# The end of the mixer: order of the vector work and of product 7's matmuls

## Chip, cores and metric

The kernel runs on one core of one Trainium2 chip. The metric is the device time of one execution in microseconds (us); three runs of the kernel before gave 1850.46 us as the median, with 1850.1 as the lowest and 1854.3 as the highest. Engines are named as the profile names them: PE is the tensor engine's matmuls, PEld its weight loads, DVE the vector engine, ACT the scalar engine, POOL GpSimd, SP the engine that issues most transfers.

## The reference

Two layers of an encoder trunk run over 512 tokens of width 1024, in float32. Each layer is a half-step feed-forward block, a mixer, and a second half-step feed-forward block:

```python
for l in range(DEPTH):
    x = x + 0.5 * swiglu(rms_norm(x, ffn1_norm[l]), ffn1_w_in[l], ffn1_w_out[l])
    x = x + mixer(rms_norm(x, mix_norm[l]), mix_w_in[l], mix_gate_bias[l], na_rpb[l],
                  na_w_out[l], f_w_out[l], mix_w_o[l])
    x = x + 0.5 * swiglu(rms_norm(x, ffn2_norm[l]), ffn2_w_in[l], ffn2_w_out[l])
return rms_norm(x, final_norm)
```

The mixer ends in `(g_na * y_na + g_f * y_f) @ w_o`, a 512x1024 by 1024x1024 product whose result is added to `x`. That product, and the start of the feed-forward block behind it, are what the change touches.

## The kernel before

**Numbers.** A float32 operand is split into a high part (ACT rounds a copy) and a low part (DVE subtracts the high part from the source, line 202 for weights, line 333 for activations). A product of two operands is three matmuls: high by high, low activation by high weight, high activation by low weight.

**Products.** `w_o` is multiplied by one level of Strassen's method, in seven half-size products numbered 1 to 7, in the order 1, 5, 2, 6, 7, 3, 4. Each has two row blocks (two PSUM banks, for example wA of product 1) and reads its weights in two granules of 128x1024 from a stream. A granule is 12 matmuls in `product`: through `late_low` the eight that read the high weight `whi` come first (lines 521 and 522, the second of them with the activation's low part) and the four that read the low weight `wlo` come last (line 524). In the first granule both row blocks run mixed, in the last one bank 0 is finished before bank 1. Products 6, 7 and 4 accumulate in the banks of product 1 (`pa`, tiles wA), product 3 in those of product 5 (`pb`, wB); product 2 has `pc` (wC).

**Adding to x.** `put(ps, i, j, sign, bs)` adds half of a bank to a quarter of `x` for the row blocks `bs`: one DVE instruction of 128x512 for a bank (line 1835). Product 7 accumulates on top of product 6 in wA, so each of its banks is free for PE only when `put` has read product 6 out of it. Product 7's activation is the difference `m01`, which DVE makes at line 1808; `parts` makes its high part m7h on ACT and its low part m7l on DVE. Product 3's parts are m3h and m3l, product 4's m4h and m4l.

**Order.** A scheduler places the instructions on every engine by priorities of its own, except where the code asks for the written order. In the block around products 6 and 7 PE and DVE keep it: `put` of pc's bank 0, product 6, `put` of both banks of product 6, `put` of pc's bank 1, product 7. Every engine runs its own queue in order.

**Weights ahead.** `whi` and `wlo` have three buffers each, so a granule's parts are made at most three granules ahead of PE. Raw weights have nine buffers in the feed-forward stage; SP issues their loads in one queue (line 148), and each waits for the buffer's last reader. Some weights are sums: of two raws on DVE (line 172), or made by a POOL transfer that accumulates onto a raw that has landed (lines 158 and 204).

**Behind the mixer.** `nxt.quad(i, j)` transposes quarters of `x` on PE (tiles tr, line 433), ACT scales them (xr) and makes the high part (xh), DVE the low part (xl, line 438). `nxt.squares` sums squares on ACT (junk). The feed-forward block's `first_block` then needs combinations of the quarters (line 616) and their parts: t5h and t5l for its product 5, t6h and t6l for its product 6. Its norm factor r is spread over the partitions by two POOL transfers, row<-r (line 512) and R<-row (line 514); DVE first reads R at line 826.

Of the kernel before, what the change touches and what calls it, by code (L numbers as in the profile page):

```python
# [31 lines left out]
AHEAD = 2  # L32
# [59 lines left out]
def encoder_kernel(  # L92
# [3 lines left out]
    V, S, G, PE = nc.vector, nc.scalar, nc.gpsimd, nc.tensor  # L96
# [15 lines left out]
    def slot(dt=F32, s="k", shape=(4, 256)):  # L112
        return kp.tile([P, *shape], dt, tag="k", name=nm(s), bufs=23)
# [8 lines left out]
    def pair(s="ps"):  # L122
        return [bank(s), bank(s)]
# [159 lines left out]
    class Stream:  # L283
# [32 lines left out]
        def next(self, ahead=AHEAD):  # L316
            self.prep(self.pos + 1 + ahead)
            it = self.items[self.pos]
            self.pos += 1
            return it.out  # L320
# [9 lines left out]
    def split(hi, lo, src, scale=None):  # L330
        if scale is None:
            S.activation(hi, src, AF.Copy)
            V.tensor_tensor(lo, src, hi.bitcast(F32), ALU.subtract)
            return
        S.activation(hi, src, AF.Copy, scale=scale)
        V.scalar_tensor_tensor(lo, src, scale, hi.bitcast(F32), ALU.mult, ALU.subtract)
# [180 lines left out]
    def late_low(parts, again=False):  # L517


        for ps, lh, ll, rh, _, start, _ in parts:  # L520
            PE.matmul(ps, lh, rh, start=start, stop=False, skip_group_check=again)  # L521
            PE.matmul(ps, ll, rh, start=False, stop=False, skip_group_check=again)  # L522
        for ps, lh, _, _, rl, _, stop in parts:
            PE.matmul(ps, lh, rl, start=False, stop=stop, skip_group_check=again)  # L524

    def product(ps, acts, kts, start, stop=True, again=False, hook=None, by_block=False, ahead=AHEAD):

        h, l, off = acts  # L530
        n = (len(kts) + 1) // 2

        def granule(i, w, b):
            res = []
            for k, kt in enumerate(kts[2 * i : 2 * i + 2]):
                c, z = slice(off + b * P, off + (b + 1) * P), slice(k * T, (k + 1) * T)
                res.append((
                    ps[b], h[:, kt, c], l[:, kt, c], w[0][:, z], w[1][:, z], start and i + k == 0,
                    stop and 2 * i + k == len(kts) - 1,
                ))  # L540
            return res

        if by_block:
            w = [ws.next() for _ in range(n)]
            for b in range(2):
                for i in range(n):
                    late_low(granule(i, w[i], b), again)
            return
        for i in range(n):
            w = ws.next(AHEAD if i < n - 1 and ahead else ahead)  # L550
            if i < n - 1:
                late_low(granule(i, w, 0) + granule(i, w, 1), again)
            else:
                late_low(granule(i, w, 0), again)
                late_low(granule(i, w, 1), again)
            if hook and i == 0:
                hook()
# [19 lines left out]
    def combo(dst, in0, in1, op, s):  # L577
        V.tensor_tensor(dst, in0, in1, op)
        return parts(dst, s)

    def parts(src, s):
        h, l = slot(F32R, s + "h"), slot(F32R, s + "l")
        split(h, l, src)
        return h, l, 0

    K4 = list(range(4))
# [41 lines left out]
    def stage_ffn(norm, nxt, late):  # L628
# [177 lines left out]
        def two(settle):  # L806

            pa = pair("A")
            product(pa, acts[1], K4, True)
            s1 = snap(pa)  # L810
            if settle:
                settle_at()
            pb = pair("B")
            product(pb, acts[5], K4, True)
            return pa, pb, s1, snap(pb)

        def second(s1):
            pc = pair("C")
            product(pc, acts[2], K4, True)
            less(pc, s1)  # L820
# [265 lines left out]
    def stage_mixer(l, norm, nxt):  # L1086
# [452 lines left out]
        with tc.manual_schedule(engines={mybir.EngineType.DVE, mybir.EngineType.Activation}):  # L1539
            with tc.manual_schedule(engines={mybir.EngineType.PE}):  # L1540
                u, k1, pa, sb, acts4 = proj_UV()
# [83 lines left out]
                low = ws.prep_high()  # L1625
# [95 lines left out]
                t12, _ = next(first)  # L1721
# [3 lines left out]
        acts = {1: (hx[0], lx[0], 0), 2: (hx[1], lx[1], 0), 3: (hx[1], lx[1], 256), 4: (hx[0], lx[0], 256)}  # L1725

        def high(src, s):
            h = slot(F32R, s + "h")
            S.activation(h, src, AF.Copy)
            return h  # L1730

        def low(h, src, s):
            l_ = slot(F32R, s + "l")
            V.tensor_tensor(l_, src, h.bitcast(F32), ALU.subtract)
            return h, l_, 0

        with tc.manual_schedule(engines={mybir.EngineType.DVE, mybir.EngineType.Activation}):
# [10 lines left out]
            w = [ws.next(), ws.next()]  # L1748
# [38 lines left out]
        m00, m01 = mq[0, 0], mq[0, 1]  # L1787
        a1 = parts(m00, "m1")
        a5 = combo(m00, m00, m01, ALU.subtract, "m5")
        w = [ws.next(), ws.next()]  # L1790
# [3 lines left out]
        pa = pair("wA")  # L1794
# [5 lines left out]
        pb = pair("wB")  # L1800
        product(pb, a5, K4, True)
        put(pb, 1, 1, -1)
        m11 = slot(F32, "mq")
        joined_words(m11, t11)
        a6 = combo(m00, m00, m11, ALU.add, "m6")
        pc = pair("wC")
        product(pc, a2, K4, True)
        V.tensor_tensor(m01, m01, m11, ALU.subtract)
        a7 = parts(m01, "m7")
        a3 = parts(m11, "m3")  # L1810
        with tc.manual_schedule(engines={mybir.EngineType.PE}):
            with tc.manual_schedule(engines={mybir.EngineType.DVE}):
                put(pc, 0, 0, 1, (0,))
                product(pa, a6, K4, False, again=True, ahead=1)
                put(pa, 0, 1, -1)
                put(pc, 0, 0, 1, (1,))
                product(pa, a7, K4, False, again=True)
                a4 = combo(m10, m10, m00, ALU.subtract, "m4")
            nxt.squares(0, 0)
            put(pa, 1, 1, 1)  # L1820
            nxt.squares(1, 1)
            nxt.quad(0, 0)
            product(pb, a3, K4, False, again=True)
        put(pb, 0, 1, 1)
        nxt.squares(0, 1)
        product(pa, a4, K4, False, again=True, hook=lambda: nxt.quad(0, 1))
# [4 lines left out]
    def put(ps, i, j, sign, bs=(0, 1)):  # L1831

        for b in bs:
            v = x[:, 2 * j + b, i * T : (i + 1) * T]
            V.scalar_tensor_tensor(v, ps[b], 0.5 * sign, v, ALU.mult, ALU.add)
# [43 lines left out]
    for l in range(L):  # L1879
        nxt = Norm(3 * l + 1)  # L1880
        stage_ffn(norm, nxt, False)
        norm, nxt = nxt, Norm(3 * l + 2)
        stage_mixer(l, norm, nxt)
        norm, nxt = nxt, Norm(3 * l + 3)
        stage_ffn(norm, nxt, l == L - 1)
        norm = nxt
# [148 lines left out]
```

## Time and profile before

| what | us |
|---|---|
| median of three runs | 1850.46 |
| the profiled execution | 1851.89 |
| its span, first to last instruction | 1850.1 |
| PE busy in the span | 1834.9 |
| DVE busy in the span | 1602.8 |
| ACT busy in the span | 1318.2 |

The profile is of one execution; a row of its timeline has the start from the span's beginning, the duration, the engine, the line and the operation with the tile written and the tiles read, and in brackets the idle time just before it with what released it. A row with x2 or more holds a group of like instructions. The mixer's end lies at about 573 to 605 us in the first layer and at about 1490 to 1522 us in the second, 917.5 us later.

### The profile page before, as it was taken

How to read it: one execution, taken by the hardware profiler on the slowest of the kernel's cores; microseconds unless marked ns; L12 is line 12 of the kernel's file. 1: busy time of each engine (PE TensorE's matmuls, PEld its weight loads, DVE VectorE, ACT ScalarE, POOL GpSimd, SP SyncE). 2: the span in 40 equal slices, each digit the busy share in tenths (PEclk: the TensorE clock that was granted, in tenths of full speed). 3: DMA queues.
4: the chain of work that ended last, by engine and by line, in shares of the span. 5: the costliest groups of instructions: out<-in, count | busy, mean ns of one | idle time of the engine just before them, and what ended most of it. 6: DMA issues, size and time to landing. Idle time of an engine off the chain costs nothing.

```text
span 1850.1 us, 24544 instructions
## 1 busy us (share of the span) xinstructions
PE 1834.9 (99%) x8834; PEld 1527.5 (83%) x8834; DVE 1602.8 (87%) x1942; ACT 1318.2 (71%) x1781; POOL 175.6 (9%) x215
## 2 busy tenths in 40 slices
PE   9999999999999999999999999999999999999998
PEld 7888888888887888888888888888888878888876
DVE  7878899787989987889998888997869899888898
ACT  6777875668576777786666778766776786677865
POOL 0001011100111010001010100101001111100010
PEclk9999999999999999999999999999999999999999
DMA  9898798934887788979888987998258878898795
GB/s 299 227 235 222 189 272 272 230 110 127 240 228 183 180 206 242 216 205 261 246 200 212 232 217 195 278 292 206 69 186 213 228 182 184 231 218 220 199 279 148
DMA packets 202538, 396.77 MB, mean 214 GB/s; under 512 B 108016, under 2 KB 108144, under 8 KB 202416
## 3 DMA queue, kind: packets, MB, share of 16 engines
q1 hardware_dynamic: 173072, 295.28, 49.8%
q0 software_dynamic: 28912, 99.38, 30.4%
q8 instruction: 69, 1.13, 0.2%
q10 hardware_dynamic: 432, 0.55, 0.1%
q14 instruction: 53, 0.43, 0.1%
HBM read 367.88 MB, written 2.11 MB: 200 GB/s over the span
## 4 chain that ended last, share of the span: by engine, by line
PE 90%; DVE 5%; DMA 3%; issue 2%; ACT 1%; POOL 0%; SPq 0%; DVEq 0%; POOLq 0%; ACTq 0%
PE A L521 10%; PE A L524 10%; PE A L522 10%; PE o L524 6%; PE o L521 5%; PE o L522 5%; PE B L521 5%; PE B L522 5%; PE B L524 5%; PE ps L326 4%; PE ps L327 3%; PE ps L328 3%; DMA raw<-in_wst_dram 3%; PE C L522 3%; PE C L521 3%; PE C L524 3%
## 5 line engine op out<-in xcount | busy, mean ns | idle before, releaser
L202 DVE TENSOR_TENSOR wlo<-raw,whi 128x1024 fp32r<-128x1024 f32 (+1 forms) x532 | 628.6, 1192 | 176.4 <-ACT whi L199 172.5
L199 ACT ACTIVATE whi<-raw 128x1024 fp32r<-128x1024 f32 (+1 forms) x532 | 544.0, 1033 | 263.9 <-PE A L522 54.0
L158 POOL DMA_DIRECT2D raw<-in_wst_dram x166 | 145.1, 897 | 1278.7 <-DMA raw<-in_wst_dram 630.6
L172 DVE TENSOR_TENSOR raw<-raw,raw 128x1024 f32<-128x1024 f32 (+1 forms) x148 | 176.3, 1192 | 2.0
L522 PE MATMUL A<-whi,xl 128*128 128x512 f32 x400 | 155.7, 389 | 0.0
L521 PE MATMUL A<-whi,xh 128*128 128x512 f32 x400 | 155.7, 389 | 0.0
L376 ACT ACTIVATE at<-zt 128x1024 uint16<-128x1024 uint16 (+2 forms) x96 | 110.3, 1166 | 11.1 <-DMA zt<-zs 10.9
L194 ACT ACTIVATE whi<-raw 128x1024 fp32r<-128x1024 f32 (+1 forms) x83 | 85.3, 1034 | 42.5 <-issue 12.8
L524 PE MATMUL A<-wlo,xh 128*128 128x512 f32 x400 | 115.0, 389 | 0.0
L195 DVE SCALAR_TENSOR_TENSOR wlo<-raw,whi 128x1024 fp32r<-128x1024 f32 (+1 forms) x83 | 98.4, 1194 | 14.2 <-ACT whi L194 14.2
L524 PEld LDWEIGHTS A<-wlo,xh 128*128 128x128 f32 x400 | 75.1, 188 | 15.6
L522 PEld LDWEIGHTS A<-whi,xl 128*128 128x128 f32 x400 | 75.1, 188 | 15.4
L521 PEld LDWEIGHTS A<-whi,xh 128*128 128x128 f32 x400 | 75.1, 188 | 15.4
L522 PE MATMUL C<-whi,xl 128*128 128x512 f32 x208 | 81.0, 389 | 0.0
L522 PE MATMUL B<-whi,xl 128*128 128x512 f32 x208 | 81.0, 389 | 0.0
L521 PE MATMUL C<-whi,xh 128*128 128x512 f32 x208 | 80.9, 389 | 0.0
L521 PE MATMUL B<-whi,xh 128*128 128x512 f32 x208 | 80.9, 389 | 0.0
L357 ACT ACTIVATE zs<-th 128x1024 uint16<-128x1024 uint16 x80 | 79.5, 1042 | 0.6 <-DVE th L766 0.6
L759 ACT ACTIVATE th<-sn,rh 128x512 f32<-128x512 f32 x80 | 55.0, 715 | 33.4 <-DVE sn L596 32.6
L591 ACT ACTIVATE sn<-A 128x512 f32<-128x512 f32 x104 | 59.0, 584 | 24.2 <-PE A L524 24.0
L524 PE MATMUL B<-wlo,xh 128*128 128x512 f32 x208 | 59.8, 389 | 0.0
L524 PE MATMUL C<-wlo,xh 128*128 128x512 f32 x208 | 59.8, 389 | 0.0
(430 smaller groups left out, 4687.4 us busy)
## 6 DMA issues: line engine op xcount, KB each, us to landing
raw<-in_wst_dram SPq DMA_DIRECT2D x468, 512.0 KB, 6.1
raw<-in_wst_dram POOLq DMA_DIRECT2D x176, 512.0 KB, 8.1
bm<-in_bias_dram SPq DMA_DIRECT2D x16, 512.0 KB, 4.1
raw<-in_wst_dram SPq DMA_DIRECT2D x30, 256.0 KB, 4.4
x<-in_xin_dram SPq DMA_DIRECT2D x4, 512.0 KB, 10.2
raw<-in_wst_dram POOLq DMA_DIRECT2D x8, 256.0 KB, 9.2
dft<-in_dft_dram POOLq DMA_DIRECT2D x8, 256.0 KB, 11.1
gb<-in_gbias_dram SPq DMA_DIRECT2D x4, 512.0 KB, 9.4
```

Source lines behind the costliest of these rows:

```text
L158: G.dma_start(out=self.t, in_=wst[GRAN_AT[self.plus]][:, 0 : self.n], accum_op=ALU.add)
L172: V.tensor_tensor(self.raw.t, self.raw.t, self.add.t, ALU.add)
L194: S.activation(hi, t, AF.Copy, scale=-1.0)
L195: self.last = V.scalar_tensor_tensor(lo, t, -1.0, hi.bitcast(F32), ALU.mult, ALU.subtract)
L199: S.activation(hi[:, cs], t[:, cs], AF.Copy)
L202: self.last = V.tensor_tensor(lo[:, cs], t[:, cs], hi[:, cs].bitcast(F32), ALU.subtract)
L326: PE.matmul(ps, lh, rh, start=start, stop=False, skip_group_check=again)
L357: S.activation(s[:, h], words[:, h], AF.Copy)
L376: S.activation(to[:, w], t[:, w], AF.Copy)
L521: PE.matmul(ps, lh, rh, start=start, stop=False, skip_group_check=again)
L522: PE.matmul(ps, ll, rh, start=False, stop=False, skip_group_check=again)
L524: PE.matmul(ps, lh, rl, start=False, stop=stop, skip_group_check=again)
```

## The change

Three things are written in another order, in both layers. First, `put` of product 6's bank 0 stands ahead of `put` of pc's bank 0, and its bank 1 right behind; product 7's low part is made only after these (its high part as before). Second, the first granule of product 7 no longer goes through `late_low` but through a new function, which runs for each row block the two high by high and the two low weight matmuls, and for both row blocks last the four that read m7l. Third, `put` of pc's bank 1 and product 3's parts follow product 7's first granule, through its hook. The number of instructions is the same on every engine.

```diff
+    def low_rows_last(blocks, again):
+
+        for parts in blocks:
+            for ps, lh, _, rh, _, start, _ in parts:
+                PE.matmul(ps, lh, rh, start=start, stop=False, skip_group_check=again)
+            for ps, lh, _, _, rl, _, _ in parts:
+                PE.matmul(ps, lh, rl, start=False, stop=False, skip_group_check=again)
+        for parts in blocks:
+            for ps, _, ll, rh, _, _, stop in parts:
+                PE.matmul(ps, ll, rh, start=False, stop=stop, skip_group_check=again)
...
-            if i < n - 1:
+            if i < n - 1 and low_last:
+                low_rows_last([granule(i, w, 0), granule(i, w, 1)], again)
+            elif i < n - 1:
                 late_low(granule(i, w, 0) + granule(i, w, 1), again)
...
-        a7 = parts(m01, "m7")
-        a3 = parts(m11, "m3")
+        h7 = high(m01, "m7")
         with tc.manual_schedule(engines={mybir.EngineType.PE}):
             with tc.manual_schedule(engines={mybir.EngineType.DVE}):
+                product(pa, a6, K4, False, again=True, ahead=1)
+                put(pa, 0, 1, -1, (0,))
                 put(pc, 0, 0, 1, (0,))
-                product(pa, a6, K4, False, again=True, ahead=1)
-                put(pa, 0, 1, -1)
-                put(pc, 0, 0, 1, (1,))
-                product(pa, a7, K4, False, again=True)
+                put(pa, 0, 1, -1, (1,))
+                a7 = low(h7, m01, "m7")
+                a3 = []
+
+                def behind_first():
+                    put(pc, 0, 0, 1, (1,))
+                    a3.append(parts(m11, "m3"))
+
+                product(pa, a7, K4, False, again=True, low_last=True, hook=behind_first)
                 a4 = combo(m10, m10, m00, ALU.subtract, "m4")
...
-            product(pb, a3, K4, False, again=True)
+            product(pb, a3[0], K4, False, again=True)
```

The scheduler answers to this in the rest of the mixer's end and in the first block of the feed-forward stage, and nowhere else. Line numbers behind the change are higher (line 1835 of `put` is 1856, line 616 is 631). Three places follow, all in the first layer; the second layer reads the same with other numbers.

The first is DVE from the difference m01 to the low part of product 3's second weight. Numbers tell the two banks of a pair apart: wA_5096 and wA_5097 are banks 0 and 1 of pa, wC_5199 and wC_5200 those of pc. Before:

```order
L1808 TENSOR_TENSOR mq_4838<-mq_4838,mq_5191 128x1024
L1835 SCALAR_TENSOR_TENSOR x<-wC_5199,x 128x512
L202 TENSOR_TENSOR wlo_5257<-raw_5026,whi_5256 128x1024
L333 TENSOR_TENSOR m7l_5242<-mq_4838,m7h_5241 128x1024
L1835 SCALAR_TENSOR_TENSOR x<-wA_5096,x 128x512
L333 TENSOR_TENSOR m3l_5246<-mq_5191,m3h_5245 128x1024
L1835 SCALAR_TENSOR_TENSOR x<-wA_5097,x 128x512
L1835 SCALAR_TENSOR_TENSOR x<-wC_5200,x 128x512
L202 TENSOR_TENSOR wlo_5290<-raw_5098,whi_5289 128x1024
L202 TENSOR_TENSOR wlo_5297<-raw_4904,whi_5296 128x1024
L202 TENSOR_TENSOR wlo_5316<-raw_4932,whi_5315 128x1024
```

After the change:

```order
L1823 TENSOR_TENSOR mq_4838<-mq_4838,mq_5191 128x1024
L202 TENSOR_TENSOR wlo_5250<-raw_5026,whi_5249 128x1024
L1856 SCALAR_TENSOR_TENSOR x<-wA_5096,x 128x512
L1856 SCALAR_TENSOR_TENSOR x<-wC_5199,x 128x512
L1856 SCALAR_TENSOR_TENSOR x<-wA_5097,x 128x512
L1749 TENSOR_TENSOR m7l_5280<-mq_4838,m7h_5241 128x1024
L202 TENSOR_TENSOR wlo_5285<-raw_5098,whi_5284 128x1024
L202 TENSOR_TENSOR wlo_5292<-raw_4904,whi_5291 128x1024
L1856 SCALAR_TENSOR_TENSOR x<-wC_5200,x 128x512
L333 TENSOR_TENSOR m3l_5309<-mq_5191,m3h_5308 128x1024
L202 TENSOR_TENSOR wlo_5316<-raw_4932,whi_5315 128x1024
```

Behind the difference, bank 0 of product 6 is read as the second instruction instead of the fourth and bank 1 as the fourth instead of the sixth; m7l goes from third to fifth, m3l from fifth to ninth, and pc's bank 1 from seventh to eighth, behind two weights that stood after it.

PE at the same place, in product 7's first granule. Before:

```order
L521 MATMUL wA_5096<-whi_5256,m7h_5241 128x512
L522 MATMUL wA_5096<-whi_5256,m7l_5242 128x512
L521 MATMUL wA_5096<-whi_5256,m7h_5241 128x512
L522 MATMUL wA_5096<-whi_5256,m7l_5242 128x512
L521 MATMUL wA_5097<-whi_5256,m7h_5241 128x512
L522 MATMUL wA_5097<-whi_5256,m7l_5242 128x512
L521 MATMUL wA_5097<-whi_5256,m7h_5241 128x512
L522 MATMUL wA_5097<-whi_5256,m7l_5242 128x512
L524 MATMUL wA_5096<-wlo_5257,m7h_5241 128x512 x2
L524 MATMUL wA_5097<-wlo_5257,m7h_5241 128x512 x2
```

After the change:

```order
L530 MATMUL wA_5096<-whi_5249,m7h_5241 128x512 x2
L532 MATMUL wA_5096<-wlo_5250,m7h_5241 128x512 x2
L530 MATMUL wA_5097<-whi_5249,m7h_5241 128x512 x2
L532 MATMUL wA_5097<-wlo_5250,m7h_5241 128x512 x2
L535 MATMUL wA_5096<-whi_5249,m7l_5280 128x512 x2
L535 MATMUL wA_5097<-whi_5249,m7l_5280 128x512 x2
```

The four matmuls that read m7l (line 535 now, 522 before) have left the front, where every second one was such, and stand last; the first four write bank 0 alone, the next four bank 1 alone.

The second place is DVE between product 4's weights and the feed-forward block's first weights, where wB_5152 and wB_5153 are product 3's two banks and xl_5348 is the low part of the first quarter. Before:

```order
L1835 SCALAR_TENSOR_TENSOR x<-wB_5152,x 128x512
L202 TENSOR_TENSOR wlo_5386<-raw_5201,whi_5385 128x1024
L438 TENSOR_TENSOR xl_5348<-xr_5349,xh_5347 128x4x256
L1835 SCALAR_TENSOR_TENSOR x<-wB_5153,x 128x512
L195 SCALAR_TENSOR_TENSOR wlo_5409<-raw_5221,whi_5408 128x1024
L195 SCALAR_TENSOR_TENSOR wlo_5442<-raw_5254,whi_5441 128x1024
L616 TENSOR_TENSOR xr_5349<-xr_5349,xr_5424 128x1024
L438 TENSOR_TENSOR xl_5348<-xr_5424,xh_5347 128x4x256
L1835 SCALAR_TENSOR_TENSOR x<-wA_5096,x 128x512
```

After the change:

```order
L1856 SCALAR_TENSOR_TENSOR x<-wB_5152,x 128x512
L1856 SCALAR_TENSOR_TENSOR x<-wB_5153,x 128x512
L202 TENSOR_TENSOR wlo_5386<-raw_5201,whi_5385 128x1024
L438 TENSOR_TENSOR xl_5348<-xr_5349,xh_5347 128x4x256
L195 SCALAR_TENSOR_TENSOR wlo_5409<-raw_5221,whi_5408 128x1024
L1856 SCALAR_TENSOR_TENSOR x<-wA_5096,x 128x512
L631 TENSOR_TENSOR xr_5349<-xr_5349,xr_5424 128x1024
L195 SCALAR_TENSOR_TENSOR wlo_5442<-raw_5247,whi_5441 128x1024
L438 TENSOR_TENSOR xl_5348<-xr_5424,xh_5347 128x4x256
```

The addition of product 3's bank 1 to x has moved two instructions up, ahead of a weight's low part and of xl; the first reader of product 4's bank 0 has moved three up, ahead of a weight (wlo_5442) and of the first combination (xr_5349).

The third place is the first feed-forward block's product 6: DVE up to its low part t6l, and POOL around the spreading of the norm factor. DVE before:

```order
L438 TENSOR_TENSOR xl_5465<-xr_5514,xh_5464 128x4x256
L348 SCALAR_TENSOR_TENSOR rt_5669<-rt_5669,ms_5665 128x4
L202 TENSOR_TENSOR wlo_5571<-raw_5366,whi_5570 128x1024
L349 SCALAR_TENSOR_TENSOR r_5668<-rt_5669,r_5668 128x4
L172 TENSOR_TENSOR raw_5312<-raw_5312,raw_5254 128x1024
L347 TENSOR_TENSOR rt_5669<-r_5668 128x4
L202 TENSOR_TENSOR wlo_5590<-raw_5293,whi_5589 128x1024
L348 SCALAR_TENSOR_TENSOR rt_5669<-rt_5669,ms_5665 128x4
L623 TENSOR_TENSOR t6l_5608<-xr_5349,t6h_5607 128x1024
L349 SCALAR_TENSOR_TENSOR r_5668<-rt_5669,r_5668 128x4
L172 TENSOR_TENSOR raw_5366<-raw_5366,raw_5287 128x1024
```

DVE after the change:

```order
L172 TENSOR_TENSOR raw_5312<-raw_5312,raw_5247 128x1024
L349 SCALAR_TENSOR_TENSOR r_5668<-rt_5669,r_5668 128x4
L202 TENSOR_TENSOR wlo_5590<-raw_5288,whi_5589 128x1024
L347 TENSOR_TENSOR rt_5669<-r_5668 128x4
L631 TENSOR_TENSOR xr_5349<-xr_5514,xr_5349 128x1024
L348 SCALAR_TENSOR_TENSOR rt_5669<-rt_5669,ms_5665 128x4
L172 TENSOR_TENSOR raw_5366<-raw_5366,raw_5282 128x1024
L349 SCALAR_TENSOR_TENSOR r_5668<-rt_5669,r_5668 128x4
L638 TENSOR_TENSOR t6l_5608<-xr_5349,t6h_5607 128x1024
L347 TENSOR_TENSOR rt_5669<-r_5668 128x4
L202 TENSOR_TENSOR wlo_5635<-raw_5312,whi_5634 128x1024
```

The sum raw_5366 stood behind t6l and now stands ahead of it, so one more full-size instruction runs before t6l. POOL before:

```order
L158 DMA raw_5531<-in_wst_dram 128x1024
L158 DMA raw_5567<-in_wst_dram 128x1024
L512 DMA row_5685<-r_5668 128x4x1
L158 DMA raw_5631<-in_wst_dram 128x1024
L514 DMA R_5466<-row_5685 128x512
L158 DMA raw_5881<-in_wst_dram 128x1024
```

POOL after the change:

```order
L158 DMA raw_5531<-in_wst_dram 128x1024
L158 DMA raw_5567<-in_wst_dram 128x1024
L158 DMA raw_5631<-in_wst_dram 128x1024
L512 DMA row_5685<-r_5668 128x4x1
L514 DMA R_5466<-row_5685 128x512
L158 DMA raw_5881<-in_wst_dram 128x1024
```

The transfer row<-r has changed places with an accumulating weight transfer (raw_5631), which is now ahead of it.

More of the change, by code (lines that the diff above doesn't have):

```diff
@@ L524, in late_low, with product @@
             PE.matmul(ps, lh, rl, start=False, stop=stop, skip_group_check=again)
-    def product(ps, acts, kts, start, stop=True, again=False, hook=None, by_block=False, ahead=AHEAD):
+    def low_rows_last(blocks, again):
[7 more added lines that the diff above has]
+                PE.matmul(ps, ll, rh, start=False, stop=stop, skip_group_check=again)
+    def product(
+        ps, acts, kts, start, stop=True, again=False, hook=None, by_block=False, ahead=AHEAD, low_last=False
+    ):
         h, l, off = acts
```

## The prediction

> **What bounds the kernel now.** I read the page's busy times first, then the chain of waits, then the waits of PE over the whole run.
>
> ```profile
> span 1850.1 us, 24544 instructions
> PE 1834.9 (99%) x8834; PEld 1527.5 (83%) x8834; DVE 1602.8 (87%) x1942; ACT 1318.2 (71%) x1781; POOL 175.6 (9%) x215
> PE 90%; DVE 5%; DMA 3%; issue 2%; ACT 1%; POOL 0%; SPq 0%; DVEq 0%; POOLq 0%; ACTq 0%
> ```
>
> PE carries nine tenths of the chain that ended last and is nearly always busy, so the kernel can only gain where PE stands still. Waits of PE on `put` are few:
>
> ```profile
> PE wA L521 <- DVE x L1835: 2.6, 4, 0.8
> PE o L524 <- DVE wlo L202: 1.3, 2, 0.7
> ...
> PE tr L433 <- DVE x L1835: 0.5, 1, 0.5
> ```
>
> (Columns: total us, times, longest.) Four waits of wA are two in each layer, both in product 7's first granule; one transpose waits. The timeline of PE shows them, first layer, then second:
>
> ```profile
> 583.82 0.61 PE L524 MATMUL wA<-wlo,m6h 128*128 128x512 f32 x2
> 585.26 0.47 PE L521 MATMUL wA<-whi,m7h 128*128 128x512 f32 x1 [0.82 <-DVE x L1835]
> 586.90 0.50 PE L521 MATMUL wA<-whi,m7h 128*128 128x512 f32 x1 [0.48 <-DVE x L1835]
> 588.88 0.39 PE L521 MATMUL wA<-whi,m7h 128*128 128x512 f32 x1
> 591.61 1.03 PE L433 MATMUL tr<-ident,x 128*128 128x128 f32 x8
> ...
> 1501.38 0.61 PE L524 MATMUL wA<-wlo,m6h 128*128 128x512 f32 x2
> 1509.10 1.03 PE L433 MATMUL tr<-ident,x 128*128 128x128 f32 x8
> ```
>
> The bracketed idle understates the loss, since a matmul's end is drawn late. By starts: product 7's second granule is 12 matmuls from 588.88 to 591.61, 0.2275 us each. Product 6's last two start at 583.82, product 7's 24 and the two make 26 x 0.2275 = 5.92 us, so the transposes were due at 589.74; they came at 591.61, **1.87 us late**. In the second layer they were due at 1507.30 and came at 1509.10, **1.80 late**. That is all that this place can give: 3.67 us.
>
> **What DVE does there.**
>
> ```profile
> 580.42 1.22 DVE L1808 TENSOR_TENSOR mq<-mq,mq 128x1024 f32<-128x1024 f32 x1
> 584.43 0.69 DVE L1835 SCALAR_TENSOR_TENSOR x<-wA,x 128x512 f32<-128x512 f32 x1
> 585.03 1.22 DVE L333 TENSOR_TENSOR m3l<-mq,m3h 128x1024 fp32r<-128x1024 f32 x1
> 586.16 0.69 DVE L1835 SCALAR_TENSOR_TENSOR x<-wA,x 128x512 f32<-128x512 f32 x1
> ```
>
> By starts, a `put` of a bank takes 0.60 us of DVE (584.43 to 585.03) and a full-size instruction 1.13 (585.03 to 586.16); results show 0.09 later. PE goes on 0.14 and 0.05 us after the shown ends of the two reads of wA (585.12 and 586.85).
>
> **Term 1, product 7's start.** The change removes nothing; it orders DVE as weight, bank 0, pc, bank 1, m7l. How fast DVE follows PE, and when product 6's bank 0 is done:
>
> ```profile
> 582.46 0.62 PE L524 MATMUL wA<-wlo,m6h 128*128 128x512 f32 x2
> ...
> 1513.66 0.61 PE L524 MATMUL wB<-wlo,m3h 128*128 128x512 f32 x2
> 1514.32 0.69 DVE L1835 SCALAR_TENSOR_TENSOR x<-wB,x 128x512 f32<-128x512 f32 x1 [1.02 <-PE wB L524]
> ```
>
> A waiting `put` starts 0.05 us after the group's end (1514.27). So: the weight from 581.55 (580.42 + 1.13) to 582.69; bank 0 at 583.08 + 0.05 = 583.13, done at 583.82; pc from 583.73; bank 1 waits for 584.43 + 0.05 = 584.48, done at 585.17; m7l from 585.08 to 586.30. PE's first matmul of product 7 is due at 583.82 + 2 x 0.2275 = 584.28, when bank 0 is free: the first wait goes. The four on bank 0 last until 585.19; bank 1 is free for PE at 585.22 to 585.31, a wait of about 0.1. The four on bank 1 end at 586.2; m7l is there at 586.35 to 586.44, a wait of 0.2. A matmul behind a stop shows 0.47 to 0.50 us in place of 0.39, 0.1 more each time, so 0.4 to 0.5 us stay. Bounds: nothing stays, or one whole `put` too much, 0.6 more. I take 0.45: **gain 1.42 and 1.35 us**.
>
> **Term 2, what is now later.** pc's bank 1 and m3l come behind two weights, with the transposes and product 3 waiting for them. In the first layer the weights behind them hang on a transfer:
>
> ```profile
> 590.23 2.23 ACT L199 ACTIVATE whi<-raw 128x1024 fp32r<-128x1024 f32 x2 [2.03 <-DMA raw<-in_wst_dram]
> ```
>
> From m7l's 586.21, two weights, `put` and m3l take 3 x 1.13 + 0.60: bank 1 of pc is added at about 589.2, m3l ready at 590.3. The transposes now want x at 590.2 and product 3 wants m3l at 591.2. Hidden, by 1 us; if a weight's raw came 1 us later, PE would lose what exceeds that. The next weight waits for the raw that lands at 590.2 in either order, so from there DVE runs as before and keeps no lead. Cost 0, bounds 0 and 0.5 a layer.
>
> **Term 3, the transposes behind product 4's first granule.**
>
> ```profile
> 597.09 0.68 DVE L1835 SCALAR_TENSOR_TENSOR x<-wB,x 128x512 f32<-128x512 f32 x1
> 600.71 0.68 DVE L1835 SCALAR_TENSOR_TENSOR x<-wB,x 128x512 f32<-128x512 f32 x1
> ...
> 600.71 0.27 PE L433 MATMUL tr<-ident,x 128*128 128x128 f32 x1
> 602.19 0.49 PE L521 MATMUL wA<-whi,m4h 128*128 128x512 f32 x1
> ...
> 1518.20 1.03 PE L433 MATMUL tr<-ident,x 128*128 128x128 f32 x8
> 1518.99 0.49 PE L521 MATMUL wA<-whi,m4h 128*128 128x512 f32 x1
> ```
>
> Eight transposes take 0.79 us in the second layer and 1.48 in the first, where they wait for product 3's bank 1: 0.69 lost. The change puts that read right behind bank 0's, at 597.7, done at 598.4; PE wants it at 600.71 - 1.42 = 599.3. **Gain 0.69**, first layer alone; bounds 0 and 0.69.
>
> **Term 4, DVE in the feed-forward block's start.**
>
> ```profile
> 610.00:640.00 30.00, 30.00 (x41) 1.00 0.73 124
> ...
> 619.53 1.22 DVE L623 TENSOR_TENSOR t6l<-xr,t6h 128x1024 fp32r<-128x1024 f32 x1
> ...
> 623.71 0.39 PE L522 MATMUL A<-whi,t6l 128*128 128x512 f32 x1
> ...
> 1536.22 1.22 DVE L623 TENSOR_TENSOR t6l<-xr,t6h 128x1024 fp32r<-128x1024 f32 x1
> 1540.51 0.39 PE L522 MATMUL A<-whi,t6l 128*128 128x512 f32 x1
> ```
>
> From 610 to 640 us DVE is busy for all 30.00 us, so it cannot follow PE's lead of 1.42 + 0.69 = 2.1 us; the lead eats slack. t6l was ready 623.71 - 620.75 = 2.96 us before PE read it, and 3.07 in the second layer. The sum that moved ahead of it costs 1.13. First layer: 2.96 - 1.13 - 2.11 = -0.28, a wait of 0.3 us. Second: 3.07 - 1.13 - 1.35 = 0.6 to spare. Cost 0.3; bounds 0 and 0.8 a layer.
>
> **Sum.** 1.42 + 1.35 + 0.69 - 0.3 = 3.16, so **3.2 us** less. The profiled execution is 1851.89, of which 1.8 lies outside the span of 1850.1; the span would be 1846.9 and that execution 1848.7. The median of the runs is 1.4 below it: 1850.46 - 3.2 = **1847.3 us**. All gains whole and no cost give 1.87 + 1.80 + 0.69 = 4.4 and 1846.1; the bad ends of terms 1 to 4 together (0.6 x 2 + 0.5 x 2 + 0.69 + 0.5 + 0.8) cost 4.2 against the sum and give 1851.5.
>
> **The rivals.**
>
> *The norm factor comes late (slower).* POOL and DVE before:
>
> ```profile
> 624.75 0.79 POOL L512 DMA_DIRECT2D row<-r  x1 [7.59 <-DVE r L349]
> 626.88 0.85 POOL L158 DMA_DIRECT2D raw<-in_wst_dram  x1 [1.34 <-ACT whi L199]
> 636.60 0.57 POOL L514 DMA_DIRECT2D R<-row  x1 [8.87 <-DMA row<-r]
> ...
> 647.53 0.69 DVE L826 TENSOR_TENSOR sn<-sn,R 128x512 f32<-128x512 f32 x1
> 649.93 1.22 DVE L202 TENSOR_TENSOR wlo<-raw,whi 128x1024 fp32r<-128x1024 f32 x1
> 655.85 1.12 PE L571 MATMUL hB<-xh,wlo 128*128 128x256 f32 x8
> ...
> raw<-in_wst_dram POOLq DMA_DIRECT2D x9, 512.0 KB, 8.4
> R<-row POOLq DMA_DIRECT2D x1, 256.0 KB, 6.5
> ```
>
> Before, 11.85 us passed from row's issue to R's, and R takes 6.5 to land: 643.1, 4.4 before its reader, with which DVE also holds up a weight that PE reads at 655.85. Now the accumulating transfer goes first. The sum that frees its raw stood right behind t6l and stands right ahead now, 1.2 us sooner: it goes at about 625.7, row at 626.6. If row's bytes run beside the accumulation as before, R lands at 644.9, before its reader at about 647.4. If they wait for all of it, 8.4 more, R lands at 653.3, the weight is ready at 653.3 + 2.4 + 1.2 = 656.9, and PE, which wants it 1.8 sooner than before, at 654.05, stops 2.85 us; 5.7 in both layers, net 2.5 slower: **1853.0**. It decides from R landing after 654.05 - 3.6 = 650.4. Against it: row took its 11 us with an accumulation issued 2 us behind it too, so the two share the engines already.
>
> The Trainium skill (DMA: Bandwidth & Descriptors, section Queues, rings and completion order) says each transfer engine takes the descriptors of one ring in ring order; by that rule the worse case holds. By the fit in its section Anatomy of one DMA, 2.0 us and 436 GB/s, the wait would be an estimated 3.2 us for 512 KB and R in time; no row quoted here shows an accumulation that short.
>
> *The gain is taken back later.* PE arrives sooner at the feed-forward stage, where raw loads follow DVE's reads, and DVE has no spare time from 610 to 640. If the slack ends at a second place like t6l, each place costs about 0.8 us a layer: two places leave 1848.9, and some 1850 if transfers set the pace. For it: DVE at 30.00 of 30. Against it: PE waits for nothing between 612 and 720 us now.
>
> *More than the waits.* If PE's waits for weights at the end of the feed-forward stages (tile o, above) went too, their 1.3 us would add to the 4.4: 1844.8. Nothing in the change reaches them but an earlier start.
>
> *The change doesn't do what it says.* DVE, in order, waits at bank 0 for PE and puts m7l behind it; if PE's release were 0.6 us rather than 0.05, product 7 would wait for bank 1 and m7l as long as now: 1850.
>
> **How the numbers follow.** Forecast, with 2 to 4.4 us gained, 0.55 (1846.0 to 1848.5); gain taken back or never made 0.20; factor late 0.15; more than the waits 0.10. A measurement of this kernel tells about 0.3% from no change, 5.6 us: below 1844.9 is faster, above 1856.0 slower. Forecast and taken-back gain lie inside. The late factor passes the bound with 1.5 us more of waiting a layer; I give it two thirds of its case, and 0.03 for a stall elsewhere in a stage whose DVE is full: slower 0.13. Faster gets most of the last case, 0.09; same 0.78. The range runs from 1844.9 to 1853.5, which leaves out part of the two outer cases.
>
> **What would show it.** Right: no wait of PE at product 7's first matmul, two short ones inside the granule, transposes some 1.4 us sooner in both layers, the second transposes of the first layer without a wait, t6l just in time. Wrong: a wait of PE of over 0.5 us on m7l or wA; a wait of DVE at the multiply by R; PE waiting on wlo between 612 and 665; or transposes waiting for pc's bank 1.

## The result, and the profile after

The changed kernel takes **1846.8 us** (median of 22 executions, 1845.0 to 1849.7) against 1850.33 (22 executions of the kernel before): ratio 0.9981, 95% interval 0.9974 to 0.9987. Two later comparisons gave 0.9983 (0.9974 to 0.9992) and 0.9988 (0.9979 to 0.9997). The forecast was 1847.3.

The page of the profiled execution (1848.62 us; before 1851.89), its span, its busy times and its chain of waits:

```profile
span 1846.8 us, 24539 instructions
PE 1835.2 (99%) x8834; PEld 1527.0 (83%) x8834; DVE 1602.3 (87%) x1942; ACT 1316.8 (71%) x1781; POOL 175.7 (10%) x215
PE 92%; DMA 3%; DVE 2%; issue 2%; ACT 1%; POOL 0%; SPq 0%; POOLq 0%; ACTq 0%; DVEq 0%
```

The work is the same: each engine's count of busy instructions is unchanged, and the five fewer in the first line are of kinds not counted there. PE's share of the chain rose from 90% to 92% and DVE's fell from 5% to 2%. The waits of PE over the whole run (total us, times, longest):

```profile
PE ps L136 <- DVE ones L132: 1.2, 1, 1.2
PE o L524 <- DVE wlo L202: 0.9, 2, 0.7
PE ps L327 <- DVE xl L438: 0.7, 1, 0.7
PE cl L521 <- ACT whi L199: 0.3, 1, 0.3
```

The four waits of wA for `put` and the one of tr are gone. Two rows were not there before. One is cl for whi, 0.3 us; waits on cl change from execution to execution (0.6 us in this trace of before, none in its second). The other is ps for xl, which comes at 1255 us, far from any edited line, and is followed up below. PE at product 7 and at the second transposes of the first layer, then at product 7 of the second:

```profile
583.66 0.62 PE L524 MATMUL wA<-wlo,m6h 128*128 128x512 f32 x2
584.12 0.61 PE L530 MATMUL wA<-whi,m7h 128*128 128x512 f32 x2
584.57 0.61 PE L532 MATMUL wA<-wlo,m7h 128*128 128x512 f32 x2
585.06 0.73 PE L530 MATMUL wA<-whi,m7h 128*128 128x512 f32 x2
585.63 0.62 PE L532 MATMUL wA<-wlo,m7h 128*128 128x512 f32 x2
586.20 1.21 PE L535 MATMUL wA<-whi,m7l 128*128 128x512 f32 x4
587.25 0.40 PE L521 MATMUL wA<-whi,m7h 128*128 128x512 f32 x1
...
590.00 1.03 PE L433 MATMUL tr<-ident,x 128*128 128x128 f32 x8
...
599.10 1.03 PE L433 MATMUL tr<-ident,x 128*128 128x128 f32 x8
599.89 0.49 PE L521 MATMUL wA<-whi,m4h 128*128 128x512 f32 x1
...
1500.04 0.62 PE L524 MATMUL wA<-wlo,m6h 128*128 128x512 f32 x2
1506.33 1.03 PE L433 MATMUL tr<-ident,x 128*128 128x128 f32 x8
```

Read by starts: from product 6's last two matmuls to the transposes it was 7.79 and 7.72 us, and is 6.34 and 6.29; free of waits it would be 5.92. The second transposes take 0.79 us, where the first layer's took 1.48. DVE in the first layer:

```profile
582.96 0.69 DVE L1856 SCALAR_TENSOR_TENSOR x<-wA,x 128x512 f32<-128x512 f32 x1 [0.31 <-PE wA L524]
583.57 0.68 DVE L1856 SCALAR_TENSOR_TENSOR x<-wC,x 128x512 f32<-128x512 f32 x1
584.32 0.69 DVE L1856 SCALAR_TENSOR_TENSOR x<-wA,x 128x512 f32<-128x512 f32 x1
584.92 1.22 DVE L1749 TENSOR_TENSOR m7l<-mq,m7h 128x1024 fp32r<-128x1024 f32 x1
586.06 2.35 DVE L202 TENSOR_TENSOR wlo<-raw,whi 128x1024 fp32r<-128x1024 f32 x2
588.33 0.69 DVE L1856 SCALAR_TENSOR_TENSOR x<-wC,x 128x512 f32<-128x512 f32 x1
588.93 1.22 DVE L333 TENSOR_TENSOR m3l<-mq,m3h 128x1024 fp32r<-128x1024 f32 x1
```

DVE now waits for PE at bank 0 (0.31 us), reads bank 1 as soon as PE leaves it, and m7l follows. In the feed-forward block behind, PE at t6l:

```profile
620.30 1.22 DVE L638 TENSOR_TENSOR t6l<-xr,t6h 128x1024 fp32r<-128x1024 f32 x1
...
621.18 0.40 PE L521 MATMUL A<-whi,t6h 128*128 128x512 f32 x1
621.57 0.50 PE L522 MATMUL A<-whi,t6l 128*128 128x512 f32 x1
621.91 0.40 PE L521 MATMUL A<-whi,t6h 128*128 128x512 f32 x1
```

The two steps are 0.39 and 0.34 us in place of 0.23: a stop of 0.27.

**Where the time went.** Matching each matmul's start with the same one's before, PE gains 1.86 us in the first layer between 583 and 660 us, and 1.44 in the second between 1500 and 1548. It gives 1.24 back between 1250 and 1265, at the wait for xl. Smaller and larger steps elsewhere, of both signs and up to 1.3 us each, add up to a further 1.2 us of gain by the last matmul; the section on the experiments takes them up.

### The profile page after: what moved, and what is told of

Its sections match the earlier page's. It is cut to its first block, busy times and chain, and to the rows that moved or that the text cites. A ratio compares the mean times of both kernels' runs of the same rounds, so it can differ in the third digit from the quotient of the medians.

```text
span 1846.8 us, 24539 instructions
## 1 busy us (share of the span) xinstructions
PE 1835.2 (99%) x8834; PEld 1527.0 (83%) x8834; DVE 1602.3 (87%) x1942; ACT 1316.8 (71%) x1781; POOL 175.7 (10%) x215
## 4 chain that ended last, share of the span: by engine, by line
PE 92%; DMA 3%; DVE 2%; issue 2%; ACT 1%; POOL 0%; SPq 0%; POOLq 0%; ACTq 0%; DVEq 0%
PE A L521 10%; PE A L524 10%; PE A L522 10%; PE o L524 6%; PE o L521 6%; PE o L522 6%; PE B L521 5%; PE B L522 5%; PE B L524 5%; PE ps L326 4%; PE ps L327 3%; PE ps L328 3%; DMA raw<-in_wst_dram 3%; PE C L522 3%; PE C L521 3%; PE C L524 3%
```

## The experiments

Durations in the table are by starts, in us. "To transposes" is from product 6's last two matmuls; "lost at 1250" is what PE loses from 1250 to 1265 us against the first trace of before.

| run | to transposes, layers 1, 2 | second transposes, layer 1 | stop at t6l, layer 1 | lost at 1250 | time | ratio to before |
|---|---|---|---|---|---|---|
| before | 7.79, 7.72 | 1.48 | 0 | - | 1850.33 | - |
| before again | 7.73, 7.79 | 1.55 | 0 | 0 | 1853.31 (one) | - |
| change | 6.34, 6.29 | 0.79 | 0.27 | 1.24 | 1846.80 | 0.9981 |
| change, 2nd | 6.29, 6.31 | 0.79 | 0.34 | 0.95 | 1847.51 | 0.9983 |
| change, 3rd | 6.30, 6.34 | 0.80 | 0.38 | 0.99 | 1847.26 | 0.9988 |
| put order alone | 7.89, 7.93 | 1.19 | 0 | 0 | 1850.44 | 1.0002 (0.9993 to 1.0011) |
| low rows alone | 7.79, 7.78 | 1.41 | 0 | 0 | 1849.99 | 0.9997 (0.9988 to 1.0006) |
| parts early | 9.77, 9.14 | 0.79 | 0 | 0 | 1854.08 | 1.0017 (1.0008 to 1.0026) |
| pb's bank alone | 7.79, 7.78 | 1.17 | 0 | 0 | 1850.30 | 0.9998 (0.9989 to 1.0006) |
| low rows later | 6.06, 6.07 | 0.79 | 0 | 0.54 | 1848.38 (one) | - |
| one copy ahead of row | 6.30, 6.30 | 0.79 | 0.27 | 0.59 | 1847.08 (one) | - |
| three copies ahead of row | 6.34, 6.30 | 0.79 | 0.90 | 0.61 | 1854.98 (one) | - |
| ch later | 6.31, 6.32 | 0.79 | 0.37 | 0 | 1847.94 | 0.9983 |
| ch later, 2nd | 6.34, 6.33 | 0.79 | 0.37 | 0 | 1847.97 | 0.9987 (0.9978 to 0.9996) |

**Both kernels once more.** No edit.

> The kernel before, unchanged, once more, to see what of the difference between two traces is only two executions. The traces of before and of the change differ at the two mixer ends by 1.87 us (layer 1, up to the second half of product t6) and 1.43 us (layer 2), and outside them by steps that nearly cancel: +1.0 at 904 us (o), -1.9 between 1188 and 1262 us, +1.3 at 1785 us, -0.8 at 1822 us. Theory: these steps are executions, not the change: this run against the first trace of before shows steps of 0.2 to 1 us at such places too, and less than 0.1 us between product 6's last matmul and the transposes (7.79 us in layer 1, 7.72 in layer 2). Rival: they belong to the change: this run then agrees with the first trace of before within 0.1 us everywhere.

> The changed kernel once more. Theory: from product 6's last two matmuls to the transposes 6.34 us in layer 1 and 6.29 in layer 2 again, within 0.05; t6l waited for in layer 1 by 0.2 to 0.3 us; outside the mixer's ends other steps than in the first trace of the change. Rival (the steps outside belong to the change): +1.0 at 904, -1.9 from 1188 to 1262, +1.3 at 1785, -0.8 at 1822 us again. Time 1846.8, 0.2% under before.

> The changed kernel a third time, beside e7_again. Theory: 6.3 us from product 6's last two matmuls to the transposes in both layers, a stop at t6l of 0.2 to 0.3 us in layer 1, a loss of 0.6 to 1.2 us between 1250 and 1265 us, ratio 0.9982.

The mixer's ends repeat within 0.08 us in both kernels. The unchanged kernel against itself shows steps of its own elsewhere (+ is a gain on the first trace): +1.23 us at 906 us, -1.15 at 1190, -1.47 at 1785, all in the attention and output products, where PE now and then waits for a weight. So a step at such a place need not come from the change; the one at 906 is before's first trace being slow there, since every other trace gains 1.0 to 1.2 us on it. The step at 1785 stays open: the three traces of the change, and the two with copies further down, all gain 1.32 us there, while the kernels with parts of the order of before scatter (before again -1.47, put order alone -0.36, low rows alone +0.83, pb's bank alone -0.54). The loss at 1250 is different: it is in all three traces of the change and in none of before.

**The two halves apart.** In the first the granule is the ordinary one; in the second DVE's order is that of before.

```diff
-                product(pa, a7, K4, False, again=True, low_last=True, hook=behind_first)
+                product(pa, a7, K4, False, again=True, hook=behind_first)
```

> The new order of VectorE's reads alone; product 7's first granule has its low rows in between, as before. Theory (the two parts only work together): bank 0 is free in time, but product 7's second matmul already reads m7l, which is there 2.5 us after product 6's last two matmuls start (586.17 - 583.66), so product 7 is held there, and from product 6's last two to the transposes it takes 2.51 + 23 x 0.2275 + 0.1 = 7.8 us, as before (7.79 and 7.72): no gain at either mixer end, the time 1850.3. Rival (the waits for wA were the loss, and the order alone takes them away): 6.3 to 6.5 us there, 1847.5. row goes ahead of the accumulating transfer here, as before: if the accumulation holds row up, row to R falls from 12.7 us by 3.2 us or more; if the two share, by 1 us or less, to 11.85.

```diff
-                product(pa, a7, K4, False, again=True)
+                product(pa, a7, K4, False, again=True, low_last=True)
```

> The low rows last alone; VectorE's order is that of before. Theory: bank 0 is read behind m7l and bank 1 behind m3l, so TensorE waits for both as before (its first matmul of product 7 1.44 us after product 6's last two, bank 1's first 3.08 us after them), and nothing that it waits for is moved: 7.7 to 7.8 us from product 6's last two to the transposes, no gain, 1850.3. Rival (the low part was what held the granule): 6.4 us there, 1847.5.

Neither gains anything. The one row of PE's waits that matters, of the put order alone and of the low rows alone:

```profile
PE wA L522 <- DVE m7l L1749: 3.4, 2, 1.7
```

```profile
PE wA L530 <- DVE x L1850: 2.6, 4, 0.8
```

With the new order alone the wait moves to m7l, one stop of 1.7 us a layer in place of two for wA; with the low rows alone the four waits for wA stand as they were (2.6 us in before too). The 1.45 us a layer exist only where nothing is waited for at both places. The first run has row ahead of the accumulation again: row to R took 10.7 us, 2.0 less than the change's 12.7. That lies between what the two theories gave, and the section on the prediction comes back to it.

**Product 3's parts left early.**

```diff
+                put(pc, 0, 0, 1, (1,))
+                a3 = [parts(m11, "m3")]
-                product(pa, a7, K4, False, again=True, low_last=True, hook=behind_first)
+                product(pa, a7, K4, False, again=True, low_last=True)
```

> The change with pc's bank 1 and product 3's low part left ahead of the weights, right behind m7l. Theory: the weight of product 7's second granule is then ready 1.73 us later (0.60 + 1.13), at 587.2 + 1.73 + 0.09 = 589.0 where TensorE wants it at 588.17: 0.85 us lost, so 7.2 us from product 6's last two matmuls to the transposes in both layers; VectorE reads product 3's bank 1 behind xl again, as before, so the second transposes of layer 1 stop for 0.4 to 0.7 us. Gain left 0.2 to 0.6 in layer 1 and 0.6 in layer 2: 1849.3. ch is free early here: no loss from 1250 to 1265 us. Rival (the parts are hidden in either place): 6.3 us there, 1847.

Worse than either theory: slower than before. DVE and PE in the first layer:

```profile
586.14 0.68 DVE L1852 SCALAR_TENSOR_TENSOR x<-wC,x 128x512 f32<-128x512 f32 x1
588.74 1.23 DVE L333 TENSOR_TENSOR m3l<-mq,m3h 128x1024 fp32r<-128x1024 f32 x1 [1.92 <-ACT m3h L332]
589.88 3.49 DVE L202 TENSOR_TENSOR wlo<-raw,whi 128x1024 fp32r<-128x1024 f32 x3
```

```profile
591.16 0.73 PE L524 MATMUL wA<-wlo,m7h 128*128 128x512 f32 x2 [2.77 <-DVE wlo L202]
```

DVE, in order, stands 1.92 us at m3l for a high part that ACT makes behind a weight whose raw landed only at about 586.1 us (ACT stood 3.25 us for it), and the weight of product 7's second granule stands behind it. PE loses 2.77 us there (1.99 in the second layer) and not 0.85. So the third part of the change is what lets the other two pay.

Not all of the loss is that stop. In the second layer PE stops there at 1507 us, and its matmuls then slow down:

```profile
1509.51 0.73 PE L524 MATMUL wA<-wlo,m7h 128*128 128x512 f32 x2 [1.99 <-DVE wlo L202]
...
1511.16 1.05 PE L524 MATMUL wA<-wlo,m7h 128*128 128x512 f32 x2
```

The trace has a granted clock of PE of 0.50 for 3.41 us in each layer, from 592.6 and from 1510.8 us, and 1.00 on both sides; the eight transposes there take 1.56 us in place of 0.79. Half of 3.41, an estimated 1.7 us, is the clock's part of the 4.7 and 3.9 us by which PE leaves the two mixers' ends later than in the change. Without it PE would still be an estimated 0.8 us a layer behind the kernel before, so the order alone already costs time.

**The read of product 3's bank 1 alone.**

```diff
-        put(pb, 0, 1, 1)
+            with tc.high_priority():
+                put(pb, 0, 1, 1)
```

> The kernel before, with the read of product 3's bank 1 ahead of xl. Theory: the second transposes of layer 1 take 0.79 us in place of 1.41 to 1.55, layer 2 as before, nothing is given back (t6l has 3 us of slack): 0.69 less, 1849.6. Rival: what is gained there is lost at xl, read by the feed-forward block's first product right behind the transposes: no gain, 1850.3.

Half: 1.17 us where 0.79 was expected. A weight stayed between the two reads, and DVE waited 0.67 us for its high part. The 0.3 us that were gained were not given back at xl; 0.3 us cannot be told in the time. In the change both reads stand side by side (596.83 us, x2), and the whole 0.69 comes.

**The low rows two matmuls later still.**

```diff
+            for parts in first:
+                low_rows_held([parts], again)
+            hook()
+            w = ws.next(ahead)
+            last = granule(1, w, 0)
...
+            for parts in first:
+                low_rows_only(parts, again)
```

> The change, with the low rows of product 7's first granule put behind the high rows of the second granule's bank 0, two matmuls later, so that nothing is left to wait for m7l. Theory (what comes last next is the second granule's weight, whose raw lands only then): ScalarE starts that weight at 585.92 us, 2.26 behind product 6's last two matmuls, and has it at 586.98; TensorE now wants it at 583.66 + 10 x 0.2275 + 0.15 = 586.09 and stops for 0.9 us, so 6.34 - 0.24 + 0.95 = 7.05 us to the transposes in layer 1; in layer 2 the weight is there at 1502.55 against 1502.47 wanted, so 6.2. No gain, the time 1847 to 1848. Rival (m7l was the last wait there): 6.1 us in both layers, 1846.5.

The rival held: 6.06 and 6.07 us, so m7l was the last wait but a short one. The theory had taken the weight that ScalarE starts at 585.9 us for the second granule's, while TensorE reads that granule's weight without waiting for it. But the scheduler also moved a weight ahead of m4l, and PE's waits have

```profile
PE wA L522 <- DVE m4l L333: 0.9, 2, 0.5
```

0.25 us a layer were gained at m7l, and by starts 0.73 and 0.79 lost at m4l: no better version.

**The table ch behind the accumulations.**

```diff
-        G.dma_start(out=ch, in_=chan)
+        with tc.issue_after(latest[0].ins):
+            G.dma_start(out=ch, in_=chan)
```

(`latest` is the accumulating transfer traced last.)

> The changed kernel, with the load of the table ch (read first after 1328 us) issued behind the two accumulating transfers that it stood ahead of on GpSimd's queue at the start of each mixer. In the two traces of the change TensorE loses 1.24 and 0.95 us between 1250 and 1265 us, waiting for xl (0.67 and 0.41 shown), and in no trace of the kernel before or of the two parts alone. There ch is issued at 1234.3 and 1233.6 us, against 1223.7 to 1224.5 in the others, and the two accumulations behind it at 1234.8 and 1235.7, against 1228.9 and 1231.3; a weight of ScalarE then waits until 1244.9, and t5l, the weight and xl of VectorE behind it come late. Theory: ch, which now waits for another buffer, blocks that queue; moved behind, the accumulations go before 1231 us, the wait for xl goes, nothing is lost between 1250 and 1265, and the time falls by about 1.1 us: 1845.7 to 1846. Rival (TensorE is simply 2 us ahead there and VectorE cannot follow): the loss stays within 0.3 us of 1.1, the time 1847.

> ch later, once more, beside the change itself on the same chip: the first look showed the loss of 0.6 to 1.2 us between 1250 and 1265 us gone, but a time like the change's. Theory: no loss there again, and 1.0 us less than the change, too little to be told in one comparison (each ratio is known to 0.09%, 1.7 us), so 0.9980 or less against 0.9983. Rival (what is saved there is lost behind it): no loss there, the same ratio as the change within 0.0003.

POOL's queue at the start of the second layer's mixer, in before, in the change, and in the second run of this kernel; then PE's stop in the change:

```profile
1224.46 0.55 POOL L1096 DMA_DIRECT2D ch<-in_chan_dram  x1 [16.95 <-DVE wlo L202]
1228.99 0.85 POOL L158 DMA_DIRECT2D raw<-in_wst_dram  x1 [3.97 <-PE o L524]
1231.31 0.86 POOL L158 DMA_DIRECT2D raw<-in_wst_dram  x1 [1.47 <-DMA raw<-in_wst_dram]
```

```profile
1234.27 0.55 POOL L1111 DMA_DIRECT2D ch<-in_chan_dram  x1 [28.96 <-DVE wlo L202]
1234.81 1.78 POOL L158 DMA_DIRECT2D raw<-in_wst_dram  x2
```

```profile
1226.20 0.86 POOL L158 DMA_DIRECT2D raw<-in_wst_dram  x1 [22.03 <-PE o L524]
1227.97 0.87 POOL L158 DMA_DIRECT2D raw<-in_wst_dram  x1 [0.90 <-DMA raw<-in_wst_dram]
1234.06 0.55 POOL L1114 DMA_DIRECT2D ch<-in_chan_dram  x1 [5.23 <-DVE wlo L204]
```

```profile
1255.74 0.50 PE L327 MATMUL ps<-xl,whi 128*128 128x512 f32 x1 [0.67 <-DVE xl L438]
```

The instructions stand in the same order in before and in the change; what differs is that ch, whose memory other weights had before it, is let go 10 us later; why that memory comes free later was not followed. With ch behind them the accumulations go at 1226 and 1228 us, and the loss at 1250 is 0 in both runs. That cause is shown. It agrees with the other runs: low rows later and the two with copies below issue ch at 1234.6 to 1238.7 us and lose 0.54 to 0.61 us, while the kernels that issue it by 1226.4 lose nothing. The time did not follow: 1847.94 and 1847.97, the change's own ratio, as the rival had it. Between 1775 and 1800 us the three traces of the change run 1.32 us ahead of before's first trace and these two only +0.14 and -0.41 (PE waits there for weights of the output product again). Whether the one causes the other is open; two traces do not tell it from the steps that before shows against itself.

**Transfers ahead of row.** One copy of 512 KB from x to DRAM between the accumulation and row, and three. Nothing reads the copies.

```diff
+            for n in range(aside):
+                other = dp.tile([P, 1024], F32, tag=f"aside{n}", name=nm("aside"))
+                with tc.issue_after(latest[0].ins):
+                    latest[0] = G.dma_start(out=other, in_=x[:, n, :])
```

> The changed kernel with one more transfer of 512 KB (a copy of part of x to DRAM that nobody reads) on GpSimd's queue, between the accumulation and row. row to R took 10.6 to 11.9 us with row first and 12.7 and 13.1 with one accumulation ahead. Theory (the transfers share the engines): 1 to 2.4 us more for each one ahead, so 14 to 15.5 us, R there at about 648.5, VectorE waits for it some 1 us and TensorE does not: time within 1 us of the change. Rival (row waits for all that is ahead on its queue): 8 us more, R there at about 655, TensorE stops for some 4 us a layer, 1855.

> Three extra transfers of 512 KB ahead of row, behind the accumulation. With one accumulation ahead row to R took 12.7, 13.1 and 14.3 us in three runs of the change's order, with one more copy ahead 13.6. Theory (what is ahead on the queue hardly holds row up): 13 to 16 us again; row itself goes 1.1 us later than with one copy, R lands at about 649, VectorE waits for it 1 to 2 us, TensorE does not. Rival (each costs its share of the engines, 1.5 us or more): 17 us or more, R at 651 to 654, TensorE stops in the block behind, 1848 to 1852.

With one copy row to R took 13.6 us in the first layer, 13.1 in the second and 14.3 in the feed-forward block between, where the copy puts an accumulation ahead of row too. DVE waited for R there by 3.04 us and in the second layer by 0.19, in the first not at all; PE lost 0.15 us in the block between, and the time was 1847.08. With three it took 15.2 in the first layer, 16.6 in the second, and 16.9 in the feed-forward block between:

```profile
649.83 0.69 DVE L851 TENSOR_TENSOR sn<-sn,R 128x512 f32<-128x512 f32 x1 [1.94 <-DMA R<-row]
...
972.84 0.69 DVE L851 TENSOR_TENSOR sn<-sn,R 128x512 f32<-128x512 f32 x1 [6.02 <-DMA R<-row]
...
976.12 1.21 PE L596 MATMUL hB<-xh,wlo 128*128 128x256 f32 x8 [0.90 <-DVE wlo L204]
```

PE does not stop behind R in the first layer, where DVE waits 1.94 us, and does so in the other two blocks, where DVE waits 6.0. The time was 1854.98, above both theories. The number is no clean price of R: the scheduler had also set sums ahead of t7l, at which PE stopped 0.8 us twice, and t6l came later (stops of 0.90 and 0.61 us by starts).

## Why the prediction was right, point by point

- **The size of the place, and term 1.** Right. It allowed 0.45 us to remain in product 7 and 0.42 and 0.37 do, in two short stops, at bank 1 of wA and at m7l, the two that it named. Gained: 1.45 and 1.43 by the two traces, against 1.42 and 1.35. The halves apart show why both were needed: m7l, read in between, would hold PE 1.7 us.
- **Term 2, pc's bank 1 and m3l later.** Right that it costs nothing: the transposes did not wait. But the prediction counted this move only as a possible cost. Left undone it costs 3.4 and 2.9 us more between product 6 and the transposes (9.77 and 9.14 against 6.3), since m3h itself comes late on ACT and, for 0.4 and 0.6 us of it, since PE's clock is then halved; the change needs it.
- **Term 3.** Right: 0.69 in the first layer, the second transposes at 0.79 us.
- **Term 4.** Right: 0.3 forecast at t6l in the first layer, 0.27 to 0.38 in three traces; none in the second.
- **The sum.** 3.16 forecast; the two places give 1.86 + 1.44 = 3.3.
- **The gain is taken back later.** In part, which the forecast had not put in: about 1 us at 1250 us. The rival had looked for it in the feed-forward stage, in DVE's full queue and at transfers paced by it; the runs showed a buffer that comes free later and blocks a queue, two blocks of work further on. With it the traces' account is 3.3 - 1.1 = 2.2 us, with nothing else counted; the measured ratios are 3.5, 3.1 and 2.2 us less, each known to 1.2 to 1.7 us, and do not tell 2.2 from 3.3. The open step at 1785 could make up for the loss. So that the time came out within 0.5 us of the forecast is in part luck: a loss of 1.1 us that the sum did not hold lies inside what the measurement can tell.
- **The norm factor late.** It did not stop PE. The premise against it was half right: row to R is 10.4 to 11.9 us in the first layer with the accumulation right behind and 12.7 to 14.3 with it ahead, so the accumulation costs about 2 us and not 8.4; R was waited for in one of the first-layer traces in which only the accumulation went ahead, by 0.76 us on DVE and not on PE. The copies show that it is a real mechanism with more ahead on the queue.

The Trainium skill (DMA: Bandwidth & Descriptors, section Queues, rings and completion order) has each transfer engine take the descriptors of a ring in order, and adds that a later one may finish its write before an earlier one; its paragraph is on the rings of SP and ACT. On GpSimd's queue here row was held up by what is ahead of it, but by about 2 us and not by all of the 8.4, which agrees with both halves. The estimate of 3.2 us from the fit in the Trainium skill (same page, section Anatomy of one DMA) was too high against these 2 us. The 436 GB/s of that fit alone, an estimated 1.2 us for 512 KB, lies among what the copies cost in the two layers, against the mean of the change's order: 0.4 and 0.9 us for one, 2.0 and 4.4 for three. The first of these is less than the 1.6 us by which that order scatters in the first layer (12.7 to 14.3).

- **More than the waits.** Not seen in the time, which stayed above the 1844.8 of this rival. By the traces it is open: the listed waits on tile o, 1.7 and 2.4 us in the two traces of before, are 0.9 us in the first trace of the change and none in the other two, but kernels without the gain have 0.9 to 1.3 as well.
- **The change does not do what it says.** No: DVE follows PE's release as read from the rows before.

## What to carry to other kernels

When an accumulator is drained and refilled, list every operand of the first matmuls behind it: the drain's order and the matmuls' order pay only together, and each tried alone showed nothing. An instruction moved behind a wait should be weighed as a gain too: what waited in line behind it (here a weight behind m3l) may be worth more than the wait that was aimed at. After an edit that leaves other orders as they were, look for waits that are new far away; a reused buffer can carry the change there.

## What the runs showed of the hardware that was not expected

- The kernel before, run twice, differs from itself in single stages by up to 1.5 us (1.23 at 906 us, 1.47 at 1785) and by 1.4 us in the span, while stages that wait for nothing repeat to 0.02 us over 270 us (matching starts from 20 to 290 us). One trace of each kernel does not assign a difference of 1 us to a cause.
- A transfer of 512 KB ahead on GpSimd's queue delayed the 2 KB transfer behind it by about 2 us when it was the accumulation, and by 0.4 to 0.9 us when it was one copy more behind that (one run, in a scatter of 1.6 us).
- Two stops of PE, 3.16 and 2.38 us from one matmul's start to the next (product 3's parts left early), were each followed by 3.41 us at a granted clock of 0.50, which began 1.3 to 1.5 us after PE had gone on. The next longest, 2.28 us at 1784 us in the second trace of before, was followed by none. The halved clock added an estimated 1.7 us to each of the two.
